# One layer on one core: gain and bias of the first norm on transposed rows, the output projection's last columns tile by tile, operands of the down projection loaded during the last pair

## The chip, the core and the metric

The kernel runs on one core of one Trainium2 chip. Its engines are PE (matmul and transposes), DVE and POOL (elementwise), ACT (activation, copies) and SP, which here issues the DMAs. The metric is device microseconds of one execution, the median of three runs.

## What is computed

One inference step of a one-layer encoder for 512 prompt rows and 128 sample rows (640 in all), with 2048 features and 8192 hidden ones. The parts that the change touches follow the two mixers:

```
mix = concatenate([y_r, y_f], axis=-1) @ w_o
h   = layer_norm(ALPHA * x + mix, ln1_g, ln1_b)      # ((z - mu) * rsqrt(var + eps)) * g + b
ffn = square(relu(h @ w_up)) @ w_down
out = layer_norm(ALPHA * h + ffn, ln2_g, ln2_b)
```

All is fp32. Each product is made of three fp32r products of high and low parts (`three`, L161): hi x hi, hi x lo, lo x hi. A high part is an ACT copy, a low part a DVE subtraction.

## The kernel before

PE's instructions stand in the order of the code. The order on the other engines and on SP's queue is set by a scheduler from its own estimates when the kernel is built; every engine, SP too, works in order, so an instruction that waits holds those behind it.

**Output projection.** The rows are five tiles of 128 (`acc0` to `acc4`), the 2048 output columns four blocks of 512 (n). Block 0, the "first columns", runs among the mixers. For blocks 1 and 2, `tokens` takes eight chunks of 256 rows of `w_o`: `split` (L234 to L239) loads 512 KB into `raw`, ACT writes `hi`, DVE writes `lo`, and PE does 30 matmuls, six for each tile, into five PSUM banks of the pool `pq`, which has five. Three raw buffers and two of each part (`SB`) are kept. `add_x` (L1177) then adds the input rows (`xz`, 256 KB each, three buffers) on DVE, which frees the bank, and takes the statistics. Block 3 is done for tiles 0 to 2 and again for tiles 3 and 4, so its weights are loaded and split twice. `layer_norm` of a tile then normalizes on ACT (L1189), multiplies by the gain on DVE (L1190), adds the bias on POOL (L1191); `hscr` keeps the rows for the residual sum (1 MB a tile).

**Transition.** h is needed transposed. The up projection is done by Strassen-like products of quarters (Winograd's form), in which `first_tokens` makes h11 and h21 (high and low parts of the transposed rows of the first 320 rows) and `sums(k)`, k from 0 to 7, makes the other five operands from four transposed pieces of 128 x 320. Between them stand `early(i, j)`, the two products of pair i (24 matmuls of 320 columns each) that need only h11 and h21, for the first three pairs (`EARLY`); their weights are two loads `we` of 256 KB.

**Pairs and down projection.** 32 pairs follow (`pair(i)`), each with seven products (A, B, C banks); their results go to `ascr`, two blocks of 128 x 640 for each pair. The down projection takes groups of eight hidden blocks; `hidden(g)` loads four `ra` (320 KB), ACT and DVE split them (`ah`, `al`); `tokens` runs over `w_down` as above; the residual rows come back from `hscr` into `acd0` to `acd4`. The hidden blocks and `w_down` are loaded after the last pair, since the pools of pairs and down projection share the space.

Of the kernel before, what the change touches and what calls it, by code (L numbers as in the profile page):

```python
# [11 lines left out]
F32 = mybir.dt.float32  # L12
# [7 lines left out]
P = 128  # L20
# [149 lines left out]
def hybrid_layer_kernel(  # L170
# [983 lines left out]
    c11p = ctx.enter_context(tc.tile_pool(name="c11p", bufs=1, reuse_waits="tile"))  # L1154
    ln = ExitStack()
# [4 lines left out]
    def tokens(w, r0, nk, n0, th, tl, k0, pts, first, last, name, tiles=range(NTT)):  # L1160

        hi, lo = split([w[r0:r0 + nk * P, n0:n0 + 512].rearrange("(k p) f -> p k f", p=P)], [P, nk, 512], name, SB)
# [17 lines left out]
    def layer_norm(z, st, g, b, pool, name):  # L1180
# [24 lines left out]
    g1 = lnp.tile([P, D], F32, name="g1", bufs=1)  # L1205
    SY.dma_start(g1, ln1_g.to_broadcast([P, D]))
    b1 = lnp.tile([P, D], F32, name="b1", bufs=1)
    SY.dma_start(b1, ln1_b.to_broadcast([P, D]))

    for tiles in ((0, 1, 2), (3, 4)):  # L1210
        pts = {t: bank(f"po3_{t}") for t in tiles}
        for s in range(8):
            tokens(w_o, s * 256, 2, 1536, yT.hi, yT.lo, 2 * s, pts,
                   s == 0, s == 7, f"o3_{s}", tiles)
        for t in tiles:
# [11 lines left out]
    HOMES = {"11": ((c11p, "c11h"), (c11p, "c11l")), "21": ((act, "th0"), (act, "tl0")), "22": ((act, "th1"), (act, "tl1")),  # L1230
             "t1": ((act, "th2"), (act, "tl2")), "t2": ((act, "th3"), (act, "tl3")), "t3": ((cmbp, "t3h"), (cmbp, "t3l")),
             "t4": ((cmbp, "t4h"), (cmbp, "t4l"))}
# [16 lines left out]
    def first_tokens(b, k0):  # L1249
        for k in range(KH):  # L1250
            pt = turn_h(bank(f"h{b}_{k}"), k0 + k, False)
            oh, ol = (x[:, k, :] for x in H[b])
            A.activation(oh, pt, AF.Copy)
            V.tensor_tensor(out=ol, in0=pt, in1=oh.bitcast(F32), op=ALU.subtract)

    def sums(k):

# [4 lines left out]
        two = [stg.tile([P, 2, HF], F32, tag="s", name=f"t{n}_{k}", bufs=4) for n in range(2)]  # L1262
        kept = two[0][:, 0, :]
# [270 lines left out]
```

## Time and profile before

| | us |
|---|---|
| median of three runs | 3379.12 |
| the three runs | 3377.31, 3379.12, 3387.83 |
| the profiled execution | 3381.56 |
| its span | 3379.8 |
| first block of the output projection after the mixers begins | 1427.21 |
| transposes of h begin | 1610.57 |
| first product of the first pair | 1697.98 |
| end of the last pair's last product (2466.92 + 3.54) | 2470.46 |

All times in the trace are counted from the start of the span. A row names the line of the kernel; L161 and L166 are helpers for all matmuls and transposes, so tiles (`po`, `pe`, `pw`, `h`, `b`) tell the stages apart.

### The profile page before, as it was taken

What the parts mean: (1) busy time and instruction counts of PE and PEld (TensorE: products, weight loads), DVE (VectorE), ACT (ScalarE), POOL (GpSimd) and SP (SyncE); (2) the same over time, 40 slices, a digit from 0 to 9 for tenths busy, and PEclk for the clock granted to TensorE, in tenths of its full rate; (3) what the DMA queues carried; (4) which work ended last, traced back from release to release, by engine and by line L of the source; (5) the groups of instructions that cost most, each with busy time, mean ns of one, the idle gap of its engine ahead of it and who ended that gap; (6) DMA issues with size and microseconds to landing.
All of it is one profiled execution on the core that took longest, in us unless ns stands there. A gap on an engine that the chain in (4) does not pass through costs nothing.

```text
span 3379.8 us, 54961 instructions
## 1 busy us (share of the span) xinstructions
PE 3229.2 (96%) x20863; PEld 2909.4 (86%) x20863; DVE 1981.1 (59%) x4900; ACT 1194.0 (35%) x2389; POOL 522.3 (15%) x841
## 2 busy tenths in 40 slices
PE   8999999999999998998789999999989999999997
PEld 7987889888898897786689999999978888888886
DVE  4487876666767584325677777777743333332335
ACT  3344444444444444312433334334332112221112
POOL 2333333232323322002300000000000000000003
PEclk9999999999999998998799999999989999999999
DMA  4342344343424344434243333333363223332232
GB/s 139 103 120 65 94 110 109 92 121 88 119 76 129 85 124 133 145 97 153 73 140 130 99 127 103 115 115 100 130 201 108 91 96 106 112 105 80 94 102 85
DMA packets 360588, 372.97 MB, mean 110 GB/s; under 512 B 42735, under 2 KB 278467, under 8 KB 358531
## 3 DMA queue, kind: packets, MB, share of 16 engines
q1 hardware_dynamic: 360178, 368.95, 35.5%
q8 instruction: 164, 2.69, 0.4%
q0 software_dynamic: 144, 0.51, 0.1%
q14 instruction: 102, 0.83, 0.1%
HBM read 306.41 MB, written 63.48 MB: 109 GB/s over the span
## 4 chain that ended last, share of the span: by engine, by line
PE 54%; DVE 2%; DMA 1%; issue 1%; ACT 0%; SPq 0%; DVEq 0%; ACTq 0%
PE pw L161 24%; PE B L161 10%; PE C L161 7%; PE A L161 6%; PE po L161 5%; PE pe L161 1%; PE pz L161 1%; DVE acc L1190 0%; DMA ra<-ascr 0%; DVE loo L239 0%; DVE acd L1494 0%; PE b L166 0%; DMA rw<-in_w_up_dram 0%; DMA raww<-in_w_down_dram 0%; PE h L166 0%
## 5 line engine op out<-in xcount | busy, mean ns | idle before, releaser
L161 PE MATMUL pw<-hiw,ah 128*128 128x512 f32 x1240 | 483.7, 390 | 14.3 <-ACT hiw L238 13.2
L161 PE MATMUL pw<-low,ah 128*128 128x512 f32 x1240 | 483.6, 390 | 0.5 <-DVE low L239 0.5
L161 PE MATMUL pw<-hiw,al 128*128 128x512 f32 x1240 | 483.3, 390 | 0.0
L239 DVE TENSOR_TENSOR low<-raww,hiw 128x1024 fp32r<-128x1024 f32 x124 | 151.9, 1225 | 419.7 <-ACT hiw L238 419.2
L238 ACT ACTIVATE hiw<-raww 128x1024 fp32r<-128x1024 f32 x124 | 131.3, 1058 | 543.3 <-PE pw L161 542.4
L161 PEld LDWEIGHTS pw<-hiw,ah 128*128 128x128 f32 x1240 | 233.4, 188 | 63.9 <-ACT hiw L238 13.4
L161 PEld LDWEIGHTS pw<-low,ah 128*128 128x128 f32 x1240 | 233.3, 188 | 49.9 <-DVE low L239 1.4
L161 PEld LDWEIGHTS pw<-hiw,al 128*128 128x128 f32 x1240 | 233.3, 188 | 48.3
L1490 POOL TENSOR_TENSOR mv<-mv,keep 128x1 f32<-128x1 f32 x5 | 7.0, 1408 | 876.4 <-DVE mv L1489 876.4
L161 PE MATMUL po<-hio,yh 128*128 128x512 f32 x320 | 132.7, 415 | 7.7 <-ACT hio L238 6.9
L161 PE MATMUL po<-loo,yh 128*128 128x512 f32 x320 | 129.1, 404 | 8.5 <-DVE loo L239 8.5
L1304 POOL TENSOR_TENSOR o<-o 128x320 f32<-128x320 f32 x29 | 20.9, 719 | 749.9 <-ACT o L1303 749.9
L161 PE MATMUL po<-hio,yl 128*128 128x512 f32 x320 | 128.0, 400 | 0.0
L1438 DVE TENSOR_TENSOR acd<-acd,pw 128x512 f32<-128x512 f32 x140 | 93.5, 683 | 57.5 <-PE pw L161 57.5
L239 DVE TENSOR_TENSOR loo<-rawo,hio 128x1024 fp32r<-128x1024 f32 (+1 forms) x48 | 56.3, 1179 | 115.2 <-ACT hio L238 115.2
L238 ACT ACTIVATE hio<-rawo 128x1024 fp32r<-128x1024 f32 (+1 forms) x48 | 43.6, 916 | 143.9 <-PE po L161 135.1
L1422 DVE TENSOR_TENSOR al<-ra,ah 128x640 fp32r<-128x640 f32 x64 | 50.5, 821 | 65.7 <-ACT ah L1421 65.7
L161 PE MATMUL B<-ht2h,hib 128*128 128x320 f32 x256 | 80.0, 313 | 8.2 <-ACT hib L1285 8.2
L1421 ACT ACTIVATE ah<-ra 128x640 fp32r<-128x640 f32 x64 | 44.6, 733 | 113.0 <-PE pw L161 60.6
L161 PEld LDWEIGHTS po<-loo,yh 128*128 128x128 f32 x320 | 62.4, 195 | 23.2 <-DVE loo L239 10.0
L161 PEld LDWEIGHTS po<-hio,yh 128*128 128x128 f32 x320 | 62.4, 195 | 22.9 <-ACT hio L238 8.2
L161 PE MATMUL B<-ht4h,hif 128*128 128x320 f32 x256 | 79.3, 310 | 2.0 <-DVE o L1379 2.0
(2445 smaller groups left out, 9864.2 us busy)
## 6 DMA issues: line engine op xcount, KB each, us to landing
rw<-in_w_up_dram SPq DMA_DIRECT2D x128, 512.0 KB
raww<-in_w_down_dram SPq DMA_DIRECT2D x124, 512.0 KB
ra<-ascr SPq DMA_DIRECT2D x64, 320.0 KB
ascr<-o SPq DMA_DIRECT2D x61, 320.0 KB
rawo<-in_w_o_dram SPq DMA_DIRECT2D x32, 512.0 KB
fscr<-fe SPq DMA_DIRECT2D x32, 320.0 KB
rawr<-in_w_in_dram SPq DMA_DIRECT2D x32, 256.0 KB
rawk<-in_w_in_dram SPq DMA_DIRECT2D x32, 256.0 KB
```

The lines of the kernel that those rows point to most:

```text
L161: self.pe.matmul(out, lhsT=lhsT, rhs=rhs, start=start, stop=stop, **more)
L238: A.activation(hi, raw, AF.Copy)
L239: V.tensor_tensor(out=lo, in0=raw, in1=hi.bitcast(F32), op=ALU.subtract)
L1304: G.tensor_tensor(out=o, in0=o, in1=o, op=ALU.mult)
L1421: A.activation(ah[f], ra, AF.Copy)
L1422: V.tensor_tensor(out=al[f], in0=ra, in1=ah[f].bitcast(F32), op=ALU.subtract)
L1438: V.tensor_tensor(out=a, in0=a, in1=pts[t], op=ALU.add)
L1490: G.tensor_tensor(out=rs, in0=rs, in1=mhalf[:, 0:1], op=ALU.pow)
```

## The change

1. `layer_norm` leaves out gain and bias. They are loaded as 32 rows of 128 (`gbr`, in one of the `xz` buffers), turned by one PE transpose behind block 2 into `gbc`, and applied to the transposed rows: in `first_tokens` by ACT on the way out of PSUM, in `sums` within the operations that make the sums. The residual rows get theirs in the down projection (`whole_norm`: 40 DVE operations of 128 x 512, eight loads).
2. The output projection has one raw buffer and four of each part (`OB`); `xz` has two buffers, not three. Block 3 runs four chunks for all tiles, keeps the other four in high and low parts, and finishes tile by tile (`last_columns`), with h11's transposes ahead of the last tile. Its weights are loaded once.
3. A fourth pair has its early products; the order of early products and sums is new.
4. Six of the eight first `ascr` blocks and the first chunk of `w_down` are loaded during the last pair (`fetch_ahead`), and their parts are made among its products.

```diff
-    def layer_norm(z, st, g, b, pool, name):
+    def layer_norm(z, st, pool, name):
...
             A.activation(z[:, c], z[:, c], AF.Identity, scale=rs[:, 0:1], bias=rs[:, 1:2])
-            V.tensor_tensor(out=z[:, c], in0=z[:, c], in1=g[:, c], op=ALU.mult)
-            G.tensor_tensor(out=z[:, c], in0=z[:, c], in1=b[:, c], op=ALU.add)
+    gbr = lnp.tile([P, 512], F32, tag="xz", name="gbr", bufs=2)[:2 * KT, :P]
+    for i, v in enumerate((ln1_g, ln1_b)):
+        SY.dma_start(gbr[KT * i:KT * i + KT, :], v.rearrange("o (k p) -> (o k) p", p=P))
...
+    OB = (1, 4, 4)
...
+    pt = dbank("gbc")
+    PE.transpose(pt[:, :2 * KT], gbr, ident[:2 * KT, :2 * KT])
+    A.activation(gbc, pt[:, :2 * KT].rearrange("p (i k) -> p i k", i=2), AF.Copy)
+
+    pts = [bank(f"po3_{t}") for t in range(NTT)]
+    for s in range(4):
+        tokens(w_o, s * 256, 2, 1536, yT.hi, yT.lo, 2 * s, pts, s == 0, False, f"o3_{s}", b=OB)
+    ends = [split([w_o[s * 256:s * 256 + 256, 1536:2048].rearrange("(k p) f -> p k f", p=P)], [P, 2, 512], f"o3_{s}", OB)
+            for s in range(4, 8)]
+
+    def last_columns(t):
+        for s, (hi, lo) in enumerate(ends):
+            for kk in range(2):
+                k = 8 + 2 * s + kk
+                ts = slice(t * P, t * P + P)
+                three(pts[t], yT.hi(k)[:, ts], yT.lo(k)[:, ts], hi[:, kk, :], lo[:, kk, :], False, k == KT - 1)
+        add_x(3, t, pts[t])
+        layer_norm(acc[t], lst[t], lnp, f"1{t}")
+        SY.dma_start(hscr[t], acc[t])
...
+            A.activation(r, pt, AF.Identity, scale=gain(k0 + k), bias=offset(k0 + k))
+            A.activation(oh, r, AF.Copy)
+            V.tensor_tensor(out=ol, in0=r, in1=oh.bitcast(F32), op=ALU.subtract)
...
+    for t in range(4):
+        last_columns(t)
+    parts("11", ((c11p, "c11h"), (c11p, "c11l")))
+    first_tokens("11", 0, range(KH))
+    first_weights = early_weights(0, 0)
+    last_columns(4)
...
-    EARLY = 3
+    EARLY = 4
...
+        def out(b, raw, shift=None):
+            oh, ol = (x[:, k, :] for x in H[b])
+            if shift is None:
+                A.activation(oh, raw, AF.Copy)
+                V.tensor_tensor(out=ol, in0=raw, in1=oh.bitcast(F32), op=ALU.subtract)
+            else:
+                A.activation(oh, raw, AF.Identity, bias=shift)
+                V.scalar_tensor_tensor(out=ol, in0=raw, scalar=shift, in1=oh.bitcast(F32), op0=ALU.add, op1=ALU.subtract)
+
+        A.activation(b12s, b12, AF.Copy, scale=gain(k))
+        A.activation(b22s, b22, AF.Copy, scale=gain(KH + k))
+        V.scalar_tensor_tensor(out=t1, in0=b11, scalar=minus[:, 0, k:k + 1], in1=b12s, op0=ALU.mult, op1=ALU.add)
+        V.tensor_tensor(out=t2, in0=b22s, in1=t1, op=ALU.subtract)
+        out("t2", t2, offset(KH + k))
+        out("t1", t1)
+        out("22", b22s, offset(KH + k))
+        V.tensor_tensor(out=t3, in0=b22s, in1=b12s, op=ALU.subtract)
+        V.scalar_tensor_tensor(out=t4, in0=b21, scalar=gain(KH + k), in1=t2, op0=ALU.mult, op1=ALU.subtract)
+        out("t3", t3, minus[:, 1, k:k + 1])
+        out("t4", t4)
...
+    early(0, 0, first_weights)
+    first_tokens("21", KH, range(KH // 2))
     early(1, 0)
+    first_tokens("21", KH, range(KH // 2, KH))
     early(2, 0)
+    early(3, 0)
     sums(0)
     early(0, 1)
     sums(1)
+    sums(2)
     early(1, 1)
-    sums(2)
+    sums(3)
+    sums(4)
     early(2, 1)
-    for k in range(3, KH):
-        sums(k)
+    sums(5)
+    sums(6)
+    early(3, 1)
+    sums(7)
...
         product(c_, sa, "t1", True, f"c{i}")
+        if i == LAST:
+            hidden(0, ahead[0:4])
...
         product(b_, w[1, 1], "t4", False, f"f{i}")
+        if i == LAST:
+            split_ahead()
+            hidden(1, ahead[4:6])
...
+    def fetch_ahead():
+
+        for n in range(2):
+            r = accp.tile([P, 3, NT], F32, tag=f"acc{n}", name=f"early{n}")
+            for k in range(3):
+                SY.dma_start(r[:, k, :], ascr[3 * n + k])
+                ahead.append(r[:, k, :])
+        w = accp.tile([P, 2, 512], F32, tag="acc4", name="earlyw")
+        SY.dma_start(w, w_down[0:2 * P, 0:512].rearrange("(k p) f -> p k f", p=P))
+        ahead.append(w)
...
+        for t in range(NTT):
+            V.tensor_tensor(out=acc[t][:, cs], in0=acc[t][:, cs], in1=gb[:, 0, :], op=ALU.mult)
+            V.tensor_tensor(out=acc[t][:, cs], in0=acc[t][:, cs], in1=gb[:, 1, :], op=ALU.add)
```

What the scheduler makes of it, at three places. The first is DVE at the boundary from block 1 to block 2. `loo2_1` is the low part of block 2's chunk 1, `xz11` the input rows of block 1 for tile 1, `po1_1` the bank of block 1 for tile 1. Before:

```order
L239 TENSOR_TENSOR loo2_0_18951<-rawo2_0_18948,hio2_0_18950 128x1024
L1177 SCALAR_TENSOR_TENSOR acc0_18592<-xz10_18923,po1_0_18610 128x512
L1177 SCALAR_TENSOR_TENSOR acc1_18593<-xz11_18927,po1_1_18611 128x512
L1178 BN_STATS lst0_18600<-acc0_18592 128x6
L1178 BN_STATS lst1_18601<-acc1_18593 128x6
L1177 SCALAR_TENSOR_TENSOR acc2_18594<-xz12_18931,po1_2_18612 128x512
L1178 BN_STATS lst2_18602<-acc2_18594 128x6
L1177 SCALAR_TENSOR_TENSOR acc3_18595<-xz13_18935,po1_3_18613 128x512
L1177 SCALAR_TENSOR_TENSOR acc4_18596<-xz14_18939,po1_4_18614 128x512
```

After:

```order
L239 TENSOR_TENSOR loo2_1_18994<-rawo2_1_18991,hio2_1_18993 128x1024
L1180 SCALAR_TENSOR_TENSOR acc0_18596<-xz10_18930,po1_0_18617 128x512
L239 TENSOR_TENSOR loo2_2_19030<-rawo2_2_19027,hio2_2_19029 128x1024
L1181 BN_STATS lst0_18604<-acc0_18596 128x6
L1180 SCALAR_TENSOR_TENSOR acc1_18597<-xz11_18934,po1_1_18618 128x512
L1181 BN_STATS lst1_18605<-acc1_18597 128x6
L1180 SCALAR_TENSOR_TENSOR acc2_18598<-xz12_18938,po1_2_18619 128x512
L1181 BN_STATS lst2_18606<-acc2_18598 128x6
```

The sums that free block 1's banks stood behind chunk 0's low part and ahead of chunk 1's; now they stand behind chunk 1's, and chunk 2's stands between the first and the second. SP's queue at the same place, before:

```order
L1176 DMA xz10_18923<-in_x_prompt_dram 128x512
L234 DMA rawo1_5_18815<-in_w_o_dram 128x2x512
L1176 DMA xz11_18927<-in_x_prompt_dram 128x512
L1176 DMA xz12_18931<-in_x_prompt_dram 128x512
L234 DMA rawo1_6_18851<-in_w_o_dram 128x2x512
L234 DMA rawo1_7_18887<-in_w_o_dram 128x2x512
L234 DMA rawo2_0_18948<-in_w_o_dram 128x2x512
L234 DMA rawo2_1_18984<-in_w_o_dram 128x2x512
L234 DMA rawo2_2_19020<-in_w_o_dram 128x2x512
L234 DMA rawo2_3_19056<-in_w_o_dram 128x2x512
L1176 DMA xz13_18935<-in_x_prompt_dram 128x512
```

After:

```order
L234 DMA rawo2_1_18991<-in_w_o_dram 128x2x512
L234 DMA rawo2_2_19027<-in_w_o_dram 128x2x512
L1179 DMA xz11_18934<-in_x_prompt_dram 128x512
L234 DMA rawo2_3_19063<-in_w_o_dram 128x2x512
L1179 DMA xz12_18938<-in_x_prompt_dram 128x512
L1179 DMA xz13_18942<-in_x_prompt_dram 128x512
L234 DMA rawo2_4_19099<-in_w_o_dram 128x2x512
L1179 DMA xz14_18946<-in_x_sample_dram 128x512
```

Before, the loads of xz10 to xz12 stood among those of block 1's chunks; now each of xz11 to xz14 stands behind a chunk of block 2. The second place is SP's queue behind the last columns; `hscr` are the stores of normalized rows, `we100` is the first half of early(1, 0)'s weights. Before:

```order
L1218 DMA hscr2_273<-acc2_18594 128x2048
L1315 DMA we000_19757<-in_w_up_dram 128x4x128
L1315 DMA we001_19759<-in_w_up_dram 128x4x128
L1315 DMA we100_19843<-in_w_up_dram 128x4x128
L1315 DMA we101_19845<-in_w_up_dram 128x4x128
L1315 DMA we200_19881<-in_w_up_dram 128x4x128
L1315 DMA we201_19883<-in_w_up_dram 128x4x128
L1218 DMA hscr3_274<-acc3_18595 128x2048
L1218 DMA hscr4_275<-acc4_18596 128x2048
L1315 DMA we010_19952<-in_w_up_dram 128x4x128
```

After:

```order
L1286 DMA we000_19649<-in_w_up_dram 128x4x128
L1286 DMA we001_19655<-in_w_up_dram 128x4x128
L1230 DMA hscr3_274<-acc3_18599 128x2048
L1230 DMA hscr4_275<-acc4_18600 128x2048
L1286 DMA we100_19775<-in_w_up_dram 128x4x128
L1286 DMA we101_19781<-in_w_up_dram 128x4x128
L1286 DMA we200_19843<-in_w_up_dram 128x4x128
```

The stores of tiles 3 and 4 stood behind all the early weights of the first products, and now stand ahead of those of the second and third pair. The third place is DVE in the second half of the last pair; `al` are low parts of the hidden blocks, `log31` those of the pair's last product, `loearly` that of the down projection's first chunk. Before:

```order
L1286 TENSOR_TENSOR lof310_28350<-rw31_0_27905,hif310_28349 128x512
L1286 TENSOR_TENSOR lof311_28366<-rw31_1_27908,hif311_28365 128x512
L1286 TENSOR_TENSOR log310_28384<-sb31_0_28168,hig310_28383 128x512
L1386 TENSOR_TENSOR o31_28165<-B31_28171,o31_28165 128x320
L1286 TENSOR_TENSOR log311_28400<-sb31_1_28169,hig311_28399 128x512
L1299 SCALAR_TENSOR_TENSOR o31_28165<-o31_28165 128x320
```

After:

```order
L1277 TENSOR_TENSOR lof310_28350<-rw31_0_27885,hif310_28349 128x512
L1277 TENSOR_TENSOR lof311_28366<-rw31_1_27888,hif311_28365 128x512
L1478 TENSOR_TENSOR al1_28390<-early1_28149,ah1_28389 128x640
L1277 TENSOR_TENSOR log310_28406<-sb31_0_28158,hig310_28405 128x512
L1478 TENSOR_TENSOR al1_28390<-early1_28149,ah1_28389 128x640
L1478 TENSOR_TENSOR al1_28390<-ra6_28395,ah1_28389 128x640
L1451 TENSOR_TENSOR o31_28155<-B31_28161,o31_28155 128x320
L1478 TENSOR_TENSOR al1_28390<-ra7_28399,ah1_28389 128x640
L1277 TENSOR_TENSOR log311_28422<-sb31_1_28159,hig311_28421 128x512
L1504 TENSOR_TENSOR loearly_28386<-earlyw_28153,hiearly_28385 128x1024
```

Four low parts of hidden blocks now stand ahead of `log311`.

## Rows read from the trace of the kernel before

**Rows 1.** The page's first part: busy time of each engine, share of the span, instructions.

```profile
PE 3229.2 (96%) x20863; PEld 2909.4 (86%) x20863; DVE 1981.1 (59%) x4900; ACT 1194.0 (35%) x2389; POOL 522.3 (15%) x841
```

**Rows 2.** Stretches of the span, all engines: start and end, length, busy time of PE, weight loads, DVE, ACT and POOL with instructions, the granted TensorE clock as a share of full speed, the busy share of the DMA engines, GB/s.

```profile
1538.00:1613.00 75.00, 63.01 (x255) 49.63 (x253) 48.25 (x48) 23.89 (x25) 22.95 (x10) 0.89 0.44 152
1613.00:1698.00 85.00, 58.50 (x277) 45.19 (x275) 53.01 (x94) 38.57 (x84) 29.74 (x25) 0.74 0.31 100
1698.00:1716.50 18.50, 17.66 (x105) 16.75 (x106) 14.77 (x25) 6.42 (x11) 0.00 (x0) 0.92 0.46 148
...
1753.60:1778.20 24.60, 24.60 (x170) 24.60 (x169) 18.17 (x31) 9.84 (x17) 0.72 (x1) 1.00 0.28 92
...
2470.40:2523.00 52.60, 37.87 (x152) 29.81 (x151) 27.19 (x33) 20.43 (x27) 0.00 (x0) 0.84 0.69 225
2523.00:3332.00 809.00, 808.96 (x3570) 669.82 (x3570) 282.10 (x320) 157.66 (x166) 0.00 (x0) 1.00 0.29 98
```

**Rows 3.** What PE waited for between 1427 and 1705: us in total, times, the longest wait.

```profile
PE po L161 <- DVE loo L239: 8.5, 3, 5.0
PE B L161 <- ACT hib L1285: 8.2, 1, 8.2
PE h L166 <- DVE h21l L1254: 6.5, 1, 6.5
PE pe L161 <- ACT hie L1285: 5.7, 3, 1.9
```

**Rows 4.** Groups of instructions between 1427 and 1580, each shape apart: line, engine, operation, tiles and shapes, count | busy us, mean ns of one | idle before it and its releaser.

```profile
L239 DVE TENSOR_TENSOR loo<-rawo,hio 128x1024 fp32r<-128x1024 f32 x27 | 32.9, 1222 | 96.2 <-ACT hio L238 96.2
L238 ACT ACTIVATE hio<-rawo 128x1024 fp32r<-128x1024 f32 x25 | 26.5, 1061 | 121.2 <-PE po L161 121.2
L1178 DVE BATCH_NORM_STATS2 lst<-acc 128x6 f32<-128x512 f32 x18 | 11.7, 682 | 0.1
L1177 DVE SCALAR_TENSOR_TENSOR acc<-xz,po 128x512 f32<-128x512 f32 x13 | 8.5, 679 | 2.2 <-DMA xz<-in_x_prompt_dram 2.2
```

**Rows 5.** The SP queue's DMA issues in order of time around 1445: start, us, engine, line, operation, tiles, count.

```profile
1445.23 0.38 SPq L234 DMA_DIRECT2D rawo<-in_w_o_dram  x1
```

**Rows 6.** Stretches of one microsecond behind that issue, with the columns of Rows 2 (the last two are the DMA engines' share and GB/s).

```profile
1445.50:1446.50 1.00, 1.00 (x6) 0.84 (x5) 0.00 (x0) 0.00 (x0) 0.00 (x0) 1.00 0.16 16
...
1447.50:1448.50 1.00, 1.00 (x6) 0.84 (x5) 0.00 (x0) 0.00 (x0) 0.00 (x0) 1.00 0.61 231
1448.50:1449.50 1.00, 1.00 (x7) 0.80 (x6) 0.00 (x0) 0.00 (x0) 0.00 (x0) 1.00 0.00 0
```

**Rows 7.** The SP queue's issues between 1478 and 1489.

```profile
1479.83 0.34 SPq L1176 DMA_DIRECT2D xz<-in_x_prompt_dram  x1
```

**Rows 8.** DVE in order of time between 1481 and 1492; in brackets the idle time before an instruction and what ended it.

```profile
1484.06 1.37 DVE L1177 SCALAR_TENSOR_TENSOR acc<-xz,po 128x512 f32<-128x512 f32 x2 [1.15 <-DMA xz<-in_x_prompt_dram]
```

**Rows 9.** The chain of waits between 1380 and 1720 in order of time: start, us, what the chain went through, number of instructions.

```profile
1427.21 146.26 PE po L161 x635
...
1610.73 3.29 PE h L166 x18
...
1631.26 9.48 PE pe L161 x48
1640.74 1.58 PE b L166 x9
...
1646.61 4.95 PE pe L161 x22
1651.56 1.58 PE b L166 x9
...
1657.36 6.23 PE pe L161 x22
...
1690.79 7.90 DMA rw<-in_w_up_dram
...
1703.87 3.52 PE C L161 x24
```

**Rows 10.** Groups of instructions between 1613 and 1700, each shape apart, columns as in Rows 4.

```profile
L1191 POOL TENSOR_TENSOR acc<-acc,b 128x1024 f32<-128x1024 f32 x4 | 11.0, 2756 | 4.7 <-PE pe L161 2.4 <-DVE acc L1190 2.3
...
L1190 DVE TENSOR_TENSOR acc<-acc,g 128x1024 f32<-128x1024 f32 x4 | 9.1, 2294 | 0.6 <-ACT acc L1189 0.6
...
L1276 POOL TENSOR_TENSOR ht4l<-t,ht4h 128x320 fp32r<-128x320 f32 x8 | 7.9, 988 | 8.9 <-ACT ht4h L1275 8.9
...
L1276 DVE TENSOR_TENSOR ht1l<-t,ht1h 128x320 fp32r<-128x320 f32 x8 | 6.1, 768 | 0.0
...
L1268 DVE TENSOR_TENSOR t<-t,b 128x320 f32<-128x320 f32 x8 | 3.8, 481 | 22.6 <-ACT h22h L1267 22.4 <-PE b L166 0.3
```

**Rows 11.** The chain of waits between 2440 and 2530, columns as in Rows 9.

```profile
2466.92 3.54 PE C L161 x24
...
2475.15 7.25 DMA raww<-in_w_down_dram
...
2484.87 9.06 PE pw L161 x29
```

**Rows 12.** Groups of instructions between 2440 and 2530, columns as in Rows 4.

```profile
L1422 DVE TENSOR_TENSOR al<-ra,ah 128x640 fp32r<-128x640 f32 x20 | 16.2, 823 | 23.4 <-ACT ah L1421 23.4
...
L239 DVE TENSOR_TENSOR low<-raww,hiw 128x1024 fp32r<-128x1024 f32 x7 | 8.6, 1225 | 2.8 <-ACT hiw L238 2.3
```

More of the change, by code (lines that the diff above doesn't have):

```diff
@@ L1158, in hybrid_layer_kernel, with tokens @@
     lnp = ln.enter_context(tc.tile_pool(name="ln1", bufs=2, reuse_waits="tile"))
-    def tokens(w, r0, nk, n0, th, tl, k0, pts, first, last, name, tiles=range(NTT)):
-        hi, lo = split([w[r0:r0 + nk * P, n0:n0 + 512].rearrange("(k p) f -> p k f", p=P)], [P, nk, 512], name, SB)
+    def tokens(w, r0, nk, n0, th, tl, k0, pts, first, last, name, tiles=range(NTT), parts=None, b=SB):
+        hi, lo = parts or split([w[r0:r0 + nk * P, n0:n0 + 512].rearrange("(k p) f -> p k f", p=P)], [P, nk, 512],
+                                name, b)
         for t in tiles:
@@ L1204, in hybrid_layer_kernel @@
             add_x(n, t, pts[t])
[L1205 to L1218, printed above, removed]
@@ new lines, in last_columns, with parts @@
+    def last_columns(t):
[7 more added lines that the diff above has]
+        SY.dma_start(hscr[t], acc[t])
+    KH = KT // 2
+    H = {}
+    def parts(b, home):
+        H[b] = [pool.tile([P, KH, HF], F32R, tag=tag, name=f"h{b}{c}") for (pool, tag), c in zip(home, "hl")]
@@ L1261, in sums @@
         b21 = turn_h(bank(f"b21_{k}"), KH + k, False)
-        two = [stg.tile([P, 2, HF], F32, tag="s", name=f"t{n}_{k}", bufs=4) for n in range(2)]
-        kept = two[0][:, 0, :]
-        raw = {"t1": two[0][:, 1, :], "t2": two[1][:, 0, :], "t3": two[1][:, 1, :], "t4": kept}
-        A.activation(kept, b12, AF.Copy)
-        oh, ol = (x[:, k, :] for x in H["22"])
-        A.activation(oh, b22, AF.Copy)
-        V.tensor_tensor(out=raw["t1"], in0=kept, in1=b11, op=ALU.subtract)
-        V.tensor_tensor(out=raw["t3"], in0=b22, in1=kept, op=ALU.subtract)
@@ L1282, in parts_w @@
-    def parts_w(src, name):
-        hi = stg.tile([P, 4, P], F32R, tag="hi", name=f"hi{name}", bufs=3)
-        lo = stg.tile([P, 4, P], F32R, tag="lo", name=f"lo{name}", bufs=2)
-        A.activation(hi, src, AF.Copy)
-        V.tensor_tensor(out=lo, in0=src, in1=hi.bitcast(F32), op=ALU.subtract)
-        return hi, lo
-    def product(pt, ws, b, start, name):
+        two = [stgu.tile([P, 2, HF], F32, tag="s", name=f"t{n}_{k}", bufs=4) for n in range(2)]
+        b12s, t1, t2, b22s = two[0][:, 0, :], two[0][:, 1, :], two[1][:, 0, :], two[1][:, 1, :]
@@ L1291, in product @@
+        out("t3", t3, minus[:, 1, k:k + 1])
+        out("t4", t4)
+    minus = cmbp.tile([P, 2, KH], F32, name="minus")
+    G.tensor_scalar(out=minus[:, 0, :], in0=gbc[:, 0, 0:KH], scalar1=-1.0, scalar2=None, op0=ALU.mult)
+    G.tensor_tensor(out=minus[:, 1, :], in0=gbc[:, 1, KH:], in1=gbc[:, 1, 0:KH], op=ALU.subtract)
+    def product(pt, ws, b, start, name, done=None):
         bh, bl = H[b]
         for q in range(2):
-            hi, lo = parts_w(ws[q], f"{name}{q}")
+            hi, lo = done[q] if done else parts_w(ws[q], f"{name}{q}")
```

147 lines of the change are left out of this document (88 added, 59 removed).

## The prediction

> **What bounds the kernel now.** The page's busy times come first: PE is busy for 96% of the span [rows 1], so time can only come from stretches in which PE waits or runs at the lower clock. The table of stretches shows where these lie [rows 2]: in the 85 us between the projection's last columns and the first pair PE is busy for 58.5 us at a mean granted clock of 0.74; in the 75 us of the last columns for 63.0 us; in the 52.6 us between the last pair and the down projection's steady part for 37.9 us at 0.84. The pairs from the fourth on (24.6 us each) and the down projection (808.96 us of 809.0) leave nothing. The same table gives the units: 3570 matmuls in 809.0 us are 0.227 us each, a chunk of 30 takes 6.8 us and a block of 240 takes 54.4 us; 24 products of 320 columns take 3.52 us [rows 9].
>
> Next I read what ended PE's waits [rows 3]: the low parts of w_o (8.5 us), the first pair's weights (8.2 us), the normalized rows through h21l (6.5 us), the early weights (5.7 us). Last the chain [rows 9]: from 1427.21 on, 635 matmuls in 146.26 us are PE alone. The reader must see this: the second and third blocks of the output projection, n=1 and n=2, have no wait now, and the change takes buffers from them.
>
> **The change, part by part: the output projection.** With one raw buffer, the next load is issued when the low part is written. The cycle is load + hi + lo. A 512 KB load issued at 1445.23 [rows 5] moves bytes until 1448.5 at the latest, and none after [rows 6]: 3.3 us. A 256 KB load issued at 1479.83 behind another [rows 7] released DVE at 1484.06 [rows 8]: 4.2 us. I take 3.6 us for a 512 KB load that runs alone, an estimate near the first row, and 4.2 us for a queued small one. With 1.06 and 1.22 us for hi and lo [rows 4] and 0.15 us of hand-over, the cycle is 6.05 us, which hides under the chunk's 6.8 us, though only 0.75 us of lead is won per chunk.
>
> The Trainium skill prices a DMA at a fixed 2.0 us plus its bytes at 436 GB/s ("DMA: Bandwidth & Descriptors", Anatomy of one DMA); for 512 KB this would be an estimate of 3.2 us. By that the lead at the end of n=1 would be some 2 us larger and the sum below 2 us smaller.
>
> *Start of n=1.* The small loads of gain and bias wait for the end of the first columns and stand on SP ahead of the first chunk; before, that chunk was there already. 3.6 + 1.06 + 0.4 us against PE's start at 1427.21 puts n=1 **3 us** later. Since the xz loads now come singly and their sums stand between the low parts on DVE, the lead begins to grow only with the fourth chunk.
>
> *End of n=1.* Four gains of 0.75 us leave lo2_1 about 1.2 us late when n=2 begins. On DVE it stands ahead of the first bank's sum; the other four sums wait for one xz load each, since gbr holds the second xz slot. Bank 1: rawo2_2 (3.6), hi, lo2_2, statistics and sum (0.68 each) [rows 4] make it free 7.3 us after lo2_1. Banks 2 to 4: a load (4.2, 2.9 to 3.2, 4.2 us) and a sum of 0.68 us each, 13 us together. The last bank is free some 21.5 us after n=2 could begin (1.2 us of lateness, 7.3, 13), and PE should have reached it after 5.4 us: a loss of **16 us**. Ends: 10 us if each load comes a microsecond sooner, 18 us if PE's clock falls.
>
> *End of n=2.* The transpose releases gbr's slot, loads are two deep, and lead is four chunks: only tiles 2 and 4 wait, **3.4 us**.
>
> *Last columns.* Now n=2 ends near 1538 (480 of the chain's 635 matmuls), and the last columns with the transposes behind them end at 1614.0 [rows 9]: 76 us. Afterwards 54.4 us of matmuls run without a wait (four chunks are kept, and tile by tile the norm of one tile is hidden by the next tile's 5.4 us), and the h11 transposes add some 4 us, paced by ACT's 0.46 us operations: 58.4 us, a **gain of 17.5 us**. The removed DVE multiplications (2.3 us) and POOL additions (2.8 us) [rows 10] are what made room.
>
> *From there to the first sums.* Before: 1614.0 to 1640.74 [rows 9], 27 us. After: the split of the first early weights stands on DVE behind tile 4's sum and statistics, so early(0,0) ends about 8 us after the last column. Then early(1,0)'s weights stand on SP behind hscr4, which waits for tile 4's norm (sum, statistics, power, two ACT halves: 8.5 us); the 1 MB store and the load need 5 us more, the split 1.3 us. early(1,0) ends 20.5 us after the last column, early(2,0) at 31 us (its load waits for the low part before it), early(3,0) at 34.5 us: **7.6 us** more. Each early product takes 4.7 to 6.2 us, not 3.5, since PE waits ahead of it and runs partly at the lower clock, as now [rows 9]. With the shifts so far the first sums start 12.5 us later than before.
>
> *Sums.* Before, a sum with an early product takes 10.75 us (1646.61 to 1657.36) [rows 9], of which DVE has 7 operations and a split. Now it is nine DVE operations of 0.48 us: 4.3 us against 3.9 us, where some of the seven were slowed, to 0.77 us, beside POOL [rows 10]. An early product stands behind two sums: 17 operations and a split before it (9.3 us), 9 transposes (1.58 us), the product (5.3 us): 16 us. 11.2 + 3 x 16 + 2.7 us to the last transpose make 62 us, where it was 49.6 us (from 1640.7 to 1690.3, half a microsecond before the first pair's loads [rows 9]): **12.3 us** more. Those loads (7.90 us) still follow the last transposes, so the pairs begin about 25 us later.
>
> *Pair 3.* Its A products are done early: it runs like the first pairs, some 18.3 us (one is the 18.5 us stretch, with a slow start) [rows 2], against 24.6 us: **gain 6.3 us**. Together the front costs 18.5 us.
>
> *Passage.* 151 matmuls of 0.227 us are 34.2 us of the 52.6 us [rows 2]; 18.4 us are to be had, mostly the wait from 2470.5 for the load of the first chunk (7.25 us from 2475.15) and what stands ahead of it [rows 11]. With operands and chunk loaded during pair 31, this goes. DVE gets eight low parts of 0.82 us and one of 1.22 us [rows 12] in a pair in which it is busy for 18.2 of 24.6 us [rows 2]; four stand ahead of the last split that product g needs, which comes some 1.5 us late. The next chunks' loads queue behind residual rows of 1 MB, and each has 3 us or more to spare; I allow 1 us. **Gain 16 us**, from 10 (one load late at each of two chunks) to 18. The gain and bias of the residual rows are 40 DVE operations of at most 0.7 us, 7 us in each block of 27.2 us, where DVE has 4 x 1.22 + 5 x 0.68 + about 3 us otherwise: free, and if that cover were gone, 3 us.
>
> Sum: 3 + 16 + 3.4 - 17.5 + 7.6 + 12.3 - 6.3 - 16 = **+2.5 us**. The profiled execution takes 3381.56 us, 2.4 us over the median of 3379.12 us; on the median the forecast is 3381.6 us.
>
> **Rivals.**
> *The transition runs at the upper clock.* If PE keeps it, eight early products cost 3.5 us and not 5.3 us: 14 us less, 3367.6 us. For it: one of the products' rows is 4.95 us for 22 [rows 9]. Against it: the mean clock of 0.74 there [rows 2], and PE has still more to wait. The boundary of n=1 at its lower end works the same way. Chance 0.22.
>
> *One raw buffer doesn't hide the load* (the slower side). Where: the 20 chunks from n=1 to the middle of n=3, lo to lo. It decides from a load of 4.4 us on, since 6.8 - 1.06 - 1.22 - 0.15 us is 4.4; at 5.0 us each chunk loses 0.65 us, 13 us in all: 3394.6 us. For it: the queued load took 4.2 us [rows 8], and the first pair's loads 7.9 us [rows 9]. Against it: nothing else is in the queue in most of these chunks, and the lone load was over after 3.3 us [rows 6]. Chance 0.16. The Trainium skill asks for two buffers so that loads overlap with work ("Trainium Kernel Development and Optimization", Best Practices). No row shows one buffer here; by that rule this rival would be the likeliest.
>
> *The passage gains 6 us only.* Fetches, residual rows and weights share the queue, which is 69% busy there now [rows 2]; if three chunk loads come 3 to 4 us late each, 10 us more, the time is 3391.6 us. For it: the load of 7.25 us [rows 11]. Against it: the fetches start a pair earlier. Chance 0.12.
>
> **How the numbers follow.** The forecast, no change that can be told, has 0.50. A measurement of this kernel tells about 0.3% (10 us) from nothing: faster is under 3369.0 us, slower over 3389.3 us. So faster 0.22, same 0.50, slower 0.28. The forecast's own range is 3370 to 3389 us; with the rivals' times and their spread, 3364 to 3396 us.
>
> **What would show it.** Right: waits of PE at the start of n=2 on the sums of add_x, up to 6 us long, 16 us together; none in the last columns; the 8 us between hscr4's store and early(1,0); pairs beginning some 25 us later than in the trace of before; three or four chunks after pair 31 with under 3 us of waits. Wrong: a wait at each chunk of n=1 and n=2 (second rival), early products near 3.5 us (first), waits <-DMA raww after pair 31 (third), or no wait at the start of n=2, which would take 16 us off the sum.

## The result and the profile after

| | before | after |
|---|---|---|
| median of four runs, us | 3380.77 | 3414.65 |
| range of the runs, us | 3377.31 to 3387.83 | 3408.42 to 3415.92 |
| span of the profiled execution, us | 3379.8 | 3414.1 |

The changed kernel is slower by 0.9%: 1.0092 times the time before, 95% interval 1.0076 to 1.0108. The forecast was 3381.6 us, its range ended at 3396 us: 33 us of the time were not foreseen.

The first part of the page of after answers to [rows 1]:

```profile
PE 3252.2 (95%) x20864; PEld 2913.9 (85%) x20864; DVE 1972.6 (58%) x4938; ACT 1200.5 (35%) x2406; POOL 474.4 (14%) x817
```

PE has one instruction more than before (the transpose of gain and bias) and is *busy* 23 us longer. Waits alone don't do that, though PE is also busy longer where its granted clock is lower behind them (0.90 in n=2). The stretches of after, with the columns of [rows 2], show where the 23 us lie:

```profile
1424.66:1432.30 7.64, 1.27 (x5) 0.60 (x5) 1.06 (x3) 3.92 (x7) 0.00 (x0) 0.74 0.32 105
1432.30:1491.85 59.55, 58.77 (x241) 46.88 (x241) 18.82 (x21) 9.54 (x9) 0.00 (x0) 0.95 0.32 102
1491.85:1562.43 70.58, 61.44 (x241) 47.77 (x241) 18.25 (x21) 9.60 (x10) 0.00 (x0) 0.90 0.30 97
1562.43:1626.72 64.29, 61.13 (x266) 47.67 (x265) 21.56 (x38) 22.11 (x31) 2.19 (x4) 1.00 0.38 132
1626.72:1660.98 34.26, 25.43 (x121) 22.46 (x121) 11.79 (x24) 15.44 (x29) 0.93 (x3) 0.80 0.35 106
1660.98:1727.60 66.62, 40.45 (x193) 32.39 (x192) 36.73 (x77) 32.45 (x68) 2.88 (x4) 0.74 0.13 40
...
2538.09:3366.02 827.93, 826.28 (x3569) 671.43 (x3568) 295.88 (x345) 156.70 (x166) 0.00 (x0) 1.00 0.29 97
```

In order: from the last transposes of the mixers to n=1; n=1; n=2; n=3 with the h11 transposes; the early products of h11; the sums; the down projection behind its first 151 matmuls. The last row matters most. In [rows 2] it was 809.0 us for 3570 matmuls, 0.227 us each; now it is 827.93 us, 0.232 us each, at a granted clock of 1.00, with PE busy for all but 1.65 us. The change adds little to that stage: ten DVE operations in each column block of its first round.

Two stretches of after within the down projection, each of 60 matmuls, show that not every matmul is longer:

```profile
2588.96:2602.57 13.61, 13.61 (x61) 11.27 (x60) 3.14 (x3) 2.15 (x3) 0.00 (x0) 1.00 0.23 77
2616.52:2630.47 13.95, 13.95 (x62) 11.30 (x60) 5.99 (x7) 4.61 (x6) 0.00 (x0) 1.00 0.52 169
```

13.61 us are 226.8 ns each, 13.95 us are 232.5 ns. The first stretch takes its stationary operand from group 0 of the hidden blocks (the home of h11, in `c11p`), the second from a group in `act`.

What PE waited for in after between 1420 and 1740, which answers to [rows 3]:

```profile
PE pe L161 <- ACT hie L1276: 29.6, 6, 7.2
PE po L161 <- DVE acc L1180: 12.3, 6, 5.2
PE B L161 <- ACT hib L1276: 10.0, 1, 10.0
PE po L161 <- ACT hio L238: 5.6, 1, 5.6
```

The second and fourth lines are the waits that the forecast had put at the boundaries of n=1 and n=2 (9.1 and 3.2 of the 12.3 us) and at the start of n=1. In n=2 the waits are only part of the loss: the third of the stretches above has PE busy for 61.44 us there, where it was 54.40 us. The first line is new: 21 of its 29.6 us are three waits of about 7.1 us in the sums. The chain of waits of after, which answers to [rows 9], names what is behind them (the pieces that the text reads; shorter ones between them are left out too):

```profile
1460.52 3.54 DMA rawo<-in_w_o_dram
1465.26 1.24 DVE loo L239
1466.51 3.50 DMA rawo<-in_w_o_dram
1471.21 1.24 DVE loo L239
...
1478.44 4.27 DMA rawo<-in_w_o_dram
...
1498.62 3.33 DMA xz<-in_x_prompt_dram
1502.76 2.65 DMA xz<-in_x_prompt_dram
1506.14 3.45 DMA xz<-in_x_sample_dram
...
1634.66 5.50 DMA we<-in_w_up_dram
...
1678.98 2.89 DMA we<-in_w_up_dram
1682.57 6.20 PE pe L161 x24
...
1696.40 2.77 DMA we<-in_w_up_dram
1699.87 6.11 PE pe L161 x24
```

With one raw buffer a chunk's cycle is 5.95 us from low part to low part (1465.26 to 1471.21; forecast 6.05), under the 6.8 us of a chunk. At the end of n=1 the xz loads come one by one. In the sums each early product hangs on a load of its weights that starts late.

Stage by stage, from the starts of the first and last matmuls (us). The trace of before has the first matmul of n=1 at 1425.95; 1427.21, given for it ahead of the prediction, is where the chain of waits enters that stage.

| stage | before | after | change | forecast |
|---|---|---|---|---|
| mixers, to their last transpose | 1420.94 | 1424.66 | +3.7 | 0 |
| to the start of n=1 | 5.01 | 7.64 | +2.6 | +3 |
| n=1 and n=2 | 111.94 | 130.13 | +18.2 | +16 |
| n=3 to the first sum | 102.78 | 98.55 | -4.2 | 3.4 - 17.5 + 7.6 = -6.5 |
| sums | 48.72 | 64.08 | +15.4 | +12.3 |
| last sum to the first pair | 8.59 | 10.28 | +1.7 | 0 |
| pairs and passage, to the 152nd matmul of the down projection | 825.06 | 802.75 | -22.3 | -6.3 - 16 = -22.3 |
| down projection | 808.92 | 827.93 | +19.0 | 0 |
| rest | 47.80 | 48.13 | +0.3 | 0 |

The mixers' code is the same. Over the twelve profiles of this study that share it their last transpose stands between 1417.24 and 1424.66, so the first line is scatter from execution to execution. Of the last 19.0 us, 2.8 us are one pause at the start of the third column block: the sums that free PE's banks stand on DVE among the products of the residual rows with their gain, and DVE waits for the load of that gain (`gb`). The forecast had these operations as free.

```profile
2558.16 3.10 DVE L1526 TENSOR_TENSOR acd<-acd,gb 128x512 f32<-128x512 f32 x5 [3.13 <-DMA gb<-in_ln_g_dram]
```

### The profile page after: what moved, and what is told of

It is laid out like the page before. It is cut to its first block, busy times and chain, and to the rows that moved or that the text cites. A ratio compares the mean times of both kernels' runs of the same rounds, so it can differ in the third digit from the quotient of the medians.

```text
span 3414.1 us, 54975 instructions
## 1 busy us (share of the span) xinstructions
PE 3252.2 (95%) x20864; PEld 2913.9 (85%) x20864; DVE 1972.6 (58%) x4938; ACT 1200.5 (35%) x2406; POOL 474.4 (14%) x817
## 4 chain that ended last, share of the span: by engine, by line
PE 56%; DMA 3%; DVE 3%; ACT 1%; issue 1%; SPq 0%; POOL 0%; DVEq 0%; ACTq 0%; POOLq 0%
PE pw L161 24%; PE B L161 10%; PE C L161 6%; PE A L161 6%; PE po L161 4%; PE pe L161 1%; DMA rawo<-in_w_o_dram 1%; DMA xz<-in_x_prompt_dram 1%; PE pz L161 1%; DMA we<-in_w_up_dram 0%; PE b L166 0%; DMA gb<-in_ln_g_dram 0%; DMA xz<-in_x_sample_dram 0%; DVE loo L239 0%; ACT hio L238 0%
## 5 line engine op out<-in xcount | busy, mean ns | idle before, releaser
L161 PE MATMUL po<-hio,yh 128*128 128x512 f32 x320 | 134.8, 421 | 18.8 <-DVE acc L1180 12.3
L239 DVE TENSOR_TENSOR loo<-rawo,hio 128x1024 fp32r<-128x1024 f32 (+1 forms) x40 | 40.4, 1009 | 112.5 <-ACT hio L238 112.5
L238 ACT ACTIVATE hio<-rawo 128x1024 fp32r<-128x1024 f32 (+1 forms) x40 | 35.5, 887 | 157.3 <-PE po L161 87.4
L161 PE MATMUL C<-ht1h,loc 128*128 128x320 f32 x256 | 79.0, 309 | 1.2 <-DVE loc L1277 1.2
L161 PE MATMUL B<-ht2h,lob 128*128 128x320 f32 x256 | 79.8, 312 | 0.2 <-DVE lob L1277 0.2
L161 PE MATMUL C<-h22h,log 128*128 128x320 f32 x256 | 79.0, 309 | 0.7 <-DVE log L1277 0.7
```

What stands on the lines that cost most here:

```text
L161: self.pe.matmul(out, lhsT=lhsT, rhs=rhs, start=start, stop=stop, **more)
L238: A.activation(hi, raw, AF.Copy)
L239: V.tensor_tensor(out=lo, in0=raw, in1=hi.bitcast(F32), op=ALU.subtract)
```

## The experiments

Two theories stood against each other for the longer matmuls. *Placement*: the tile `gbc` (128 bytes per partition) is the first in its pool and moves everything behind it, the moving operands `hio` and `hiw` among them, by 128 bytes, while `yh` and most of the hidden blocks, in an older pool, stay where they were. *Waits*: operands come a little late at every chunk.

**e1_pad**: the changed kernel with the tile padded.

```
-    gbc = accp.tile([P, 2, KT], F32, name="gbc")
+    gbc = accp.tile([P, 4, KT], F32, name="gbc")[:, 0:2, :]
```

> The changed kernel with the gain-and-bias tile padded from 128 to 256 bytes per partition; nothing else differs. Theory (placement): in the changed kernel the 512-column matmuls take 232.3 ns instead of 226.7 because the 128-byte tile moved the moving operands (hio, hiw) by 128 bytes against the stationary ones (yh, ah1 to ah4). With 256 bytes both stand as before modulo 256: every matmul of the projection's blocks and of the down projection is back at about 227 ns, about 4 us come back in the 720 matmuls of the projection, 19 us in the down projection, and the time is about 3391 us. Rival (waits alone): the matmuls are long because chunks or banks come late; the pad changes nothing, 3414 us, 232 ns.

Measured: 3391.12 us, 1.003 times before (1.002 to 1.004). Its stretches of n=1, n=2 and the down projection, columns as above:

```profile
1430.90:1489.59 58.69, 57.43 (x241) 46.69 (x241) 18.82 (x21) 9.54 (x9) 0.00 (x0) 0.95 0.32 103
1489.59:1557.22 67.63, 59.06 (x241) 46.80 (x241) 18.25 (x20) 9.61 (x10) 0.00 (x0) 0.92 0.31 102
...
2533.51:3343.84 810.33, 809.63 (x3569) 669.43 (x3568) 296.14 (x345) 156.61 (x166) 0.00 (x0) 1.00 0.30 100
```

The down projection is back at 810.33 us, 17.6 us less than in after; n=1 and n=2 give back 0.9 and 2.95 us: 21.4 us in these stretches, from 128 unused bytes. The medians of the two kernels lie 23.5 us apart, their ratios to before 0.62% or 21 us. Placement stands; the 1.4 us that 810.33 has over 808.92 are the pause for `gb` again, which is 1.2 us shorter here than in after.

**e2_shift**: the kernel before, with the same 128 bytes and nothing else.

```
+    off = accp.tile([P, 32], F32, name="off")
+    G.memset(off, 0.0)
     ln = ExitStack()
```

> The kernel before with an unused tile of 128 bytes per partition ahead of the accumulators, which moves hio and hiw by 128 bytes against yh and ah1 to ah4; no instruction of the loops differs. Theory (placement): the matmuls with yh and ah1 to ah4 as stationary operands go from 226.7 to about 232.3 ns, those with ah0 (which moves along) stay; about 23 us slower than before, 3404 us. Rival (waits alone): no change, 3381 us.

Measured: 3397.43 us, 1.005 (1.0033 to 1.0067), 15.8 us more than before on the same chip. The expectation of 23 us was too high in size: the down projection is 16.4 us longer, as the first row below shows, n=1, n=2 and n=3 4 us together, and the mixers of the profiled execution ran 2.2 us shorter. The second and third rows are 60 matmuls each, with group 0 of the hidden blocks and with a group in `act`.

```profile
2522.53:3347.85 825.32, 825.32 (x3569) 671.82 (x3569) 282.16 (x320) 157.80 (x166) 0.00 (x0) 1.00 0.29 96
2570.80:2584.41 13.61, 13.61 (x62) 11.26 (x60) 3.14 (x3) 2.16 (x3) 0.00 (x0) 1.00 0.23 77
2584.41:2598.36 13.95, 13.95 (x62) 11.31 (x61) 8.05 (x10) 4.75 (x7) 0.00 (x0) 1.00 0.51 170
```

PE is busy for the whole stretch: there is no wait in it, the matmuls themselves are longer. This rules the rival out.

**e7_s64** and **e8_s256**: as e2_shift with `[P, 16]` and `[P, 64]`, to see which distance counts.

> The kernel before with an unused tile of 64 bytes (not 128) ahead of the accumulators. If only the remainder modulo 128 counts, or any difference costs, the matmuls with ah1 to ah4 take 232 ns as with 128 bytes; if the cost belongs to a difference of 128 bytes, they take about 227 ns.

> The kernel before with an unused tile of 256 bytes ahead of the accumulators. Theory (modulo 256): all matmuls of the down projection at 226.7 ns, time as before. Rival (the shift itself, or modulo 512 and more): 232 ns, 3397 us.

Measured, in one run each: 3386.87 and 3382.48 us. The down projection of the one with 64 bytes:

```profile
2521.60:3336.78 815.18, 815.18 (x3568) 670.13 (x3569) 282.38 (x320) 157.61 (x166) 0.00 (x0) 1.00 0.29 97
```

and of the one with 256 bytes:

```profile
2523.99:3332.87 808.88, 808.88 (x3569) 669.77 (x3569) 282.30 (x320) 157.44 (x166) 0.00 (x0) 1.00 0.29 98
```

256 bytes cost nothing. 64 bytes cost 6.3 us, which neither of the two cases expected: the mean interval from matmul to matmul in a chunk is 228.9 ns with 64 bytes, 232.2 to 232.7 ns with 128, 226.7 ns with 0 and 256. In e2_shift and e7_s64 the chunks of the group that moves along with `hiw` keep 226.6 to 227.0 ns (two of 46 have 227.7 and 227.9). Their operands have both moved and they are not slower; the others' stationary operands have not moved and they are. So the difference between the two operands' addresses counts, not either address. That it counts modulo 256 fits all four differences tried, and the 512-byte steps between the stationary operands of a chunk, which change nothing.

**e3_gbr**: as e1_pad, with the second buffer of xz left to the input rows.

```
-    gbr = lnp.tile([P, 512], F32, tag="xz", name="gbr", bufs=2)[:2 * KT, :P]
+    gbr = stgu.tile([P, 2, HF], F32, tag="s", name="gbr", bufs=4)[:2 * KT, 0, :P]
```

> As the padded kernel, and the tile that receives gain and bias (gbr) stands in a stage buffer that is free at that time, so that the residual rows (xz) have both of their buffers in n=1. Theory of the prediction (the 16 us at the end of n=1 come largely from residual loads that come singly): the block n=2 takes 55 to 62 us and not 70.6, 8 to 14 us less than the padded kernel, about 3380 us. Rival (the banks wait for the DVE's order and for lo parts with one raw buffer, whatever the xz buffers): under 4 us less.

Measured: 3378.37 us, 0.9989 (0.998 to 0.9999), 12.7 us less than e1_pad. Of this, the start of n=1 gives 3.25 us (5.00 us after the mixers, as before). n=1 and n=2 together take 123.5 us against 126.3 us; the bank waits of n=2 are gone, but one of 6.8 us ahead of it is left, in the first of these rows (n=1, n=2):

```profile
1422.24:1487.60 65.36, 57.15 (x241) 46.50 (x241) 20.40 (x23) 10.61 (x10) 0.00 (x0) 0.92 0.31 102
1487.60:1545.74 58.14, 57.88 (x242) 46.76 (x242) 17.54 (x21) 8.55 (x9) 0.00 (x0) 0.95 0.35 113
```

So the second xz buffer is worth 2.8 us here, not 8 to 14: the rival was right on that boundary. n=3 up to the first sum gives 6.4 us, with the waits at its start gone. The spans of the two profiles differ by 5.4 us more, which is the mixers' scatter and not in the medians.

**e6_two_raw** went at the wait that is left; it stands on **e5_order** (below), and has two raw buffers.

```
-    OB = (1, 4, 4)
+    OB = (2, 3, 3)
...
-    for s in range(4):
+    for s in range(5):
         tokens(w_o, s * 256, 2, 1536, ...)
-            for s in range(4, 8)]
+            for s in range(5, 8)]
...
-                k = 8 + 2 * s + kk
+                k = 10 + 2 * s + kk
```

> As the reordered kernel, with two raw, three high and three low buffers for w_o in place of one, four and four, and three chunks of the last columns kept for the tile by tile part in place of four. Theory of the prediction (one raw buffer leaves little lead, so that the chunk at the boundary of n=1 comes late): the wait of 6.8 us ahead of the first matmul of n=2 falls under 3 us, 3 to 6 us less than the reordered kernel. Rival (the wait at n=2 comes from the order on DVE, bank sums behind low parts, whatever the loads): the wait stays at 5 us or more, no gain.

Measured: 3354.43 us against 3361.83 us of e5_order on the same chip, 7.4 us less where 3 to 6 were expected, and 3351.94 us when it was run again (**e6_again**).

> The same kernel as the one with two raw buffers, on the chip of the next two, so that they can be compared: 3354 us.

n=1 and n=2 of e5_order:

```profile
1427.17:1491.88 64.71, 57.03 (x241) 46.42 (x241) 20.17 (x23) 10.60 (x10) 0.00 (x0) 0.92 0.31 102
1491.88:1549.90 58.02, 57.69 (x241) 46.77 (x241) 17.53 (x21) 8.55 (x9) 0.00 (x0) 0.95 0.35 113
```

and of e6_two_raw:

```profile
1423.56:1481.30 57.74, 57.28 (x240) 46.85 (x241) 20.71 (x24) 9.38 (x9) 0.00 (x0) 0.95 0.38 124
1481.30:1535.97 54.67, 54.67 (x243) 45.01 (x241) 15.89 (x18) 8.56 (x9) 0.00 (x0) 1.00 0.31 104
```

The wait is gone, with 10.3 us of the two blocks in these traces (7.4 us between the medians of the whole), and both are again within 0.3 us of before:

```profile
1425.95:1483.49 57.54, 57.08 (x241) 46.70 (x241) 20.59 (x25) 8.31 (x8) 0.00 (x0) 0.95 0.37 121
1483.49:1537.89 54.40, 54.40 (x242) 45.06 (x240) 15.94 (x18) 8.49 (x8) 0.00 (x0) 1.00 0.31 102
```

With both xz buffers in place, what was left of the loss at the boundary is the missing lead of one raw buffer.

**e5_order**: as e3_gbr, and in the sums the weights of a product are loaded and split between its two sums, not behind them. The instructions are the same.

```
-    sums(1)
-    sums(2)
-    early(1, 1)
...
+    for i in range(1, 4):
+        sums(2 * i - 1)
+        ws = early_weights(i, 1)
+        sums(2 * i)
+        early(i, 1, ws)
```

> As the kernel with gbr in a stage buffer, and in the sums the early weights of a product are loaded and split between the two sums that stand ahead of it, not behind them (same instructions, another order). Theory (weight loads): the three waits of about 7.1 us for the early weights there come from loads that can only start when the second sum frees a stage buffer; with the load earlier each shrinks to under 2.5 us, the stretch from the first to the last transpose of the sums goes from 63 to about 50 us, and the time is 10 to 14 us less, about 3366 us. Rival (the prediction's account: 9 DVE operations of 0.48 us per sum set the pace): the waits turn into waits of the transposes or the split for DVE, the stretch stays above 59 us, 3374 us or more.

Measured: 3361.83 us, 0.994 (0.9923 to 0.9957), 16.5 us less than e3_gbr (by ratios to before 0.49%, 16.6 us). The stretch of the sums went from 63.16 to 49.02 us:

```profile
1642.46:1691.48 49.02, 39.96 (x192) 32.27 (x192) 33.40 (x72) 32.02 (x65) 2.88 (x4) 0.79 0.14 43
```

DVE is busy for 33.4 of these 49 us. Its rows in after show what it did in the old order (DVE in order of time, as in [rows 8]):

```profile
1678.41 0.54 DVE L1330 SCALAR_TENSOR_TENSOR ht3l<-t,minus,ht3h 128x320 fp32r<-128x320 f32 x1
...
1682.55 0.69 DVE L1277 TENSOR_TENSOR loe<-we,hie 128x512 fp32r<-128x512 f32 x1 [1.15 <-ACT hie L1276]
...
1683.56 0.69 DVE L1277 TENSOR_TENSOR loe<-we,hie 128x512 fp32r<-128x512 f32 x1
1690.44 0.55 DVE L1334 SCALAR_TENSOR_TENSOR t<-b,minus,t 128x320 f32<-128x320 f32 x1 [6.19 <-PE b L166]
```

The load `we` is issued at 1678.98, right when t3's low part has released a stage buffer of the first of two sums; PE waits for the weights until 1682.57 and then does the product; DVE has nothing to do for 6.19 us, since the next transposes stand behind that product on PE. The two engines took turns. With the load earlier they overlap; PE's waits there are three of 2.17 us for DVE.

**e9_ahead**: as e6_two_raw, with the raw weights of early(1,0) loaded ahead of the last tile's columns, so that they don't stand on SP behind its store (`early_loads` is the part of `early_weights` that issues the loads).

```
     first_weights = early_weights(0, 0)
+    second = early_loads(1, 0)
     last_columns(4)
...
-    early(1, 0)
+    early(1, 0, early_weights(1, 0, second))
```

> As the kernel with two raw buffers, but the raw weights of early(1,0) are loaded before the last tile's columns and not behind that tile's store to hscr. Theory of the prediction (these weights stand on SP behind the store, which waits for the norm): the wait of 4.3 us ahead of early(1,0) falls under 1.5 us, and the time is 3 to 4 us less. Rival (the split of these weights waits for the low buffers of early(0,0) anyway): the wait stays above 3 us, under 1 us less.

Measured: 3349.26 us, 0.9904 (0.9885 to 0.9923), against 0.9912 (0.9895 to 0.993) of e6_again on the same chip. The wait ahead of early(1,0) is gone, and the stretch from the last column to the first sum is 27.40 us, where it was 34.05 us. In e6_again it was:

```profile
1610.82 0.64 PE L161 MATMUL pe<-h11h,hie 128*128 128x320 f32 x1 [4.29 <-ACT hie L1276]
```

The medians differ by 2.7 us, which lies within their intervals (the mixers of the one profiled execution ran 3.3 us longer than of the other): the trace shows the mechanism, the times don't settle its worth.

**e10_first**: as e9_ahead, with 96 unused bytes in the mixers' staging pool, which puts `hio0`, the moving operand of the first columns, at a difference of 0 from `yh`.

```
+    off = stg.tile([P, 24], F32, name="off")
+    G.memset(off, 0.0)
```

> As the kernel before it, and a pad of 96 bytes in the attention's staging pool, by which the high and low parts of the first columns of w_o (hio0) stand like yh modulo 256. Theory (placement, in a place where PE has to wait for the attention anyway): the 240 matmuls of the first columns go from about 233 to 227 ns, and the time changes by less than 2 us. Rival (PE sets the pace there): 1.4 us less in that stretch and all of it in the time; or, if the pad disturbs the 320-column matmuls of the attention, slower.

Measured: 3342.41 us, 0.9886 (0.9871 to 0.9901), 6.9 us less than e9_ahead, though the intervals overlap. The matmuls of the first columns that follow one another without a gap went from 233.4 to 229.5 ns on average, about half of them to 227 as expected, and the 320-column matmuls of the mixers from 146.8 to 146.4 ns. Some 240 of the one and 4800 of the other make 0.9 + 1.9 us, less than the 6.9 us. The rest is not explained: in the two profiled executions 8.1 of the 9.1 us between them lie in the mixers, whose scatter alone is 7 us.

**e4_passage**: the kernel before with the change's passage alone (`fetch_ahead`, `split_ahead`, `hidden` inside the last pair) and every operand placed as before.

```
...
+        if i == LAST:
+            fetch_ahead()
         pair(i, here)
...
```

> The kernel before with only the passage of the change: operands and first chunk of the down projection loaded and split inside the last pair, the placement of operands as before. Theory: this part gains the 16 to 18 us that its row shows in the changed kernel (18.2 us there), and 512-column matmuls stay at 227 ns: 3381 - 16 = 3365 us. Rival (the gain is given back later, in residual rows and chunk loads that queue): 3375 us or more.

Measured: 3368.05 us, 0.9962 (0.9947 to 0.9977): 13.5 us faster than before by the medians. In its trace the first pair to the 152nd matmul of the down projection takes 16.1 us less than before and the rest of the down projection 808.74 us, so nothing of it is given back later:

```profile
2508.69:3317.43 808.74, 808.74 (x3569) 669.67 (x3568) 281.07 (x320) 156.69 (x166) 0.00 (x0) 1.00 0.29 97
```

## Why the prediction was wrong

**The step that failed** stands in the first part: "3570 matmuls in 809.0 us are 0.227 us each, a chunk of 30 takes 6.8 us and a block of 240 takes 54.4 us". The number was read rightly, and then carried over to the changed kernel as a constant. That "the down projection (808.96 us of 809.0) leave nothing" was true of gains and silently taken for losses too. No term of the sum had room for a matmul of another length. What the runs showed in its place: 512-column matmuls of 232.2 to 232.7 ns instead of 226.7, wherever the change had moved one operand by 128 bytes against the other. The padded kernel shows what it cost, 21.4 us in the three stretches compared (23.5 us by the medians), of the 32 us between the sum's +2.5 us and the +34 us of the trace. The range could not hold it: the slower rivals were all late loads. Most of the rest are the scatter of the mixers (3.7 us), the sums (3.1), the last columns with what follows (2.3) and the part of the pause for `gb` that the padded kernel keeps (1.4); the prediction had the operations with `gb` as free.

**The sums** were right in size by accident. The prediction counted 17 DVE operations ahead of each product and got 16 us for two sums and a product, where the trace shows 17.3 us (1682.57 to 1699.87). But DVE was not the bound: the same operations in another order take 14 us less. Loads that wait for a buffer had been counted for the products before the sums, and not here.

**The boundary of n=1** came out near the forecast of +16 us, with 14.4 us in the padded kernel, whose matmuls have their old length (n=1 and n=2: 126.32 against 111.94 us), but its parts did not, so the size is partly luck. The prediction had 16 us of waits on the bank sums; in n=2 of the padded kernel PE waits for 8.6 us on them and is busy 4.7 us longer than before, at a mean granted clock of 0.92. And of its two causes, it gave the late low parts 8.5 us (1.2 + 7.3) and the xz loads that come singly 13, less 5.4 us of cover; taken away one after the other, the single xz loads were worth 2.8 us and then the one raw buffer 10.3. The other order was not run. The cycle under one raw buffer, 6.05 us, is 5.95 us in the trace. The 3.2 us that the prediction worked out from the Trainium skill for a 512 KB load were too low: lone loads took 3.50 to 3.57 us, and the section cited there is about DMAs that GpSimd issues, while these are SP's.

**Start of n=1** (+3; +2.6) was right, and its cause too: e3_gbr, in which the small loads ahead of the first chunk go to a buffer that is free, starts n=1 as before. **Last columns** and what follows (-6.5; -4.2) were forecast 2.3 us too good. The forecast of the weights behind hscr4 is confirmed by e9_ahead. **Pair 3 and the passage** (-22.3) came out at -22.3, and the passage alone gains 16.1 us in the trace of e4_passage (13.5 us by the medians; forecast 16).

**The rivals.** That the transition keeps the upper clock fell: the granted clock is 0.80 and 0.74 in its two stretches, as the forecast had it. That one raw buffer doesn't hide the load fell in the form given, a loss at each chunk: a load took 3.5 us when alone and 4.27 us (1478.44) at most in the chain of n=1, under the 4.4 us from which it decides. What a second buffer buys is lead for the boundary. There the advice of the Trainium skill to use two buffers ("Trainium Kernel Development and Optimization", Best Practices) holds, with 10.3 us as its number in these traces. That the passage gains 6 us only fell with e4_passage.

**The mechanism behind the longer matmuls** is not settled. The runs show on what they depend, not why. In the down projection's traces the load of the next weights starts about 3 ns behind the start of a matmul and takes 188 ns. That the read of the moving operand and this read of the weights get in each other's way at some distances would fit, but is only argued. With 64 bytes the intervals follow the three products (229.2, 231.7 and 225.8 ns, again and again); with 128 bytes they run from 228 to 241 ns in a pattern that repeats every seven matmuls, so no one product carries the cost. The Trainium skill speaks against such a collision: it gives weight loads a second, independent read port ("SBUF — State Buffer", the section on a bandwidth-pool intuition that's wrong). Read that way, the placement should not matter; here it costs 5.6 ns of 226.7, and the measurement decides.

## What to carry to other kernels

When PE has no waits and is busy longer for the same instructions, compare the time of one matmul before looking for stalls, and then the addresses: a small tile placed first in a pool moves everything behind it. For matmuls like these, keep such tiles at multiples of 256 bytes per partition, or put them last. A buffer that hides its load within the steady chunk can still cost ten microseconds at a boundary where other loads and sums join the queue, and an engine that is "busy all the time" by a count of its operations should be looked at in the trace, since two engines that take turns look like one that is slow. With the tile padded, the buffers given back and the loads moved ahead, the change makes 3342 to 3354 us (0.989 to 0.992 of before); as written it loses 0.9%.

## What the hardware showed that was not expected

| difference of the moving and the stationary operand's address, modulo 256 bytes | ns of a 512-column matmul in the down projection |
|---|---|
| 0 (before, e1_pad, e8_s256) | 226.7 |
| 64 (e7_s64) | 228.9 |
| 128 (after, e2_shift) | 232.2 to 232.7 |

The granted clock is 1.00 in all of these stretches. The 320-column matmuls of the mixers, moved by 96 bytes in e10_first, changed far less (146.8 to 146.4 ns). Other differences were not tried in the down projection.
